# Transposed right-side sums and a Strassen opening for the up matrix

## The chip, the cores and the metric

The kernel runs on one core of one Trainium2 chip. The metric is the device time of one execution in microseconds (us), the median of three runs. The engines have these names in the profile: PE is the tensor engine (matrix products and transposes into PSUM), DVE the vector engine, ACT the scalar engine, POOL the GpSimd engine, SP the engine that issues most DMAs. SBUF is the working memory, PSUM the eight banks into which TensorE adds up its products.

## The reference, cut to what matters

One decoder layer on 1024 rows of width 1024. The change touches only the two gated feed-forward blocks, one at the start and one at the end:

```python
def swiglu(h, w_gate, w_up, w_down):
    return (jax.nn.silu(h @ w_gate) * (h @ w_up)) @ w_down

x = x + 0.5 * swiglu(rms_norm(x, g_ffn1), w1_gate, w1_up, w1_down)
...   # projections, two attentions, gates, output projection
x = x + 0.5 * swiglu(rms_norm(x, g_ffn2), w2_gate, w2_up, w2_down)
```

The gate and up matrices are 1024 x 2816, all in float32.

## The kernel before

**Numbers.** A float32 operand is held as two fp32r parts, high and low (`halve`, L375 to L379: the scalar engine copies the high part, POOL or the vector engine subtracts it to get the low part). A block product (`times`, L465 to L471) is four steps over the inner dimension with three matmuls each: 12 matmuls of 128x128 by 512 columns into one PSUM bank.

**Feed-forward, first half** (`ffn_in`, L446). The weights are the left side, taken two blocks of 128 columns at a time, so eleven pairs p, for gate (e = 0) and up (e = 1). Each left side is cut into four blocks A11, A12, A21, A22 (two column blocks, two halves of the inner dimension). The right side is the normalised input, transposed, cut into B11, B21 (rows 0 to 511 of x) and B12, B22 (rows 512 to 1023). In pairs 1 to 10, `products` (L477) takes seven Strassen products in place of eight block products; `FACTORS` (L371) gives their operands, with S1 to S4 from the left blocks (`left_sides`, L452) and T1 to T4 from the right ones. T1 = B12 - B11, T2 = B22 - T1, T3 = B22 - B12, T4 = B21 - T2.

**The opening** (`opening`, L501) is pair 0, where the right side isn't ready yet. It is written out by hand for TensorE, DVE, ACT and POOL: the `manual_schedule` block keeps each engine in program order. Before the change both matrices are multiplied there with eight plain block products each (`half(e, r, c, q)`), column by column of the result, and `gated` multiplies silu of gate (`gate`) with up. Between the products stand the turns: `Right.turn` (L419) makes one right-side operand out of 16 TensorE transposes of rows into four PSUM banks and four high and four low parts. T1 to T4 are formed in the row layout (`Right.sum`, L430, four subtractions each) and then turned as B12 and B22 are. B11 and B21 are turned ahead of the products: in the first block right there, in the second one inside the output projection before it (`between`, L2112). `Right.stat` and `Right.norm` (L405, L411) normalise a row tile.

**What sets the order around it.** The eight PSUM banks are four letters with two buffers each (`banks`, L323). A new tile of a letter waits until an older one has been read for the last time. Left-side operands come from nine tiles in turn (`op`), weights as loaded from four (`raw`), the transposed operands from 28 (`tt`), working tiles of 512 columns from `ct` and `sums`. Outside the hand-written opening a planner orders each engine's instructions. `lefts` (L596) loads and splits the left side of the next product group, called as `nxt` within the opening. `finish` (L587) forms the operands of the second half and stores them. The second half (`ffn_out`, L618) multiplies with the down matrix in four passes. Between the two feed-forward blocks lie the projections and the attentions, about 670 to 1540 us.

Of the kernel before, what the change touches and what calls it, by code (L numbers as in the profile page):

```python
# [11 lines left out]
F32R = mybir.dt.float32r  # L12
# [45 lines left out]
def f32(ap):  # L58
    return ap.bitcast(F32)
# [186 lines left out]
def trunk(ctx, tc, x, positions, g_ffn1, w1_gate, w1_up, w1_down, g_mix, w_in, g_cq, w_uq_a, w_q_idx,  # L246
# [134 lines left out]
    class Right:  # L381
# [4 lines left out]

        ROWS = {"B11": (0, 0), "B21": (0, 1), "B12": (1, 0), "B22": (1, 1), "T1": (0, 0), "T2": (0, 0), "T3": (0, 0),
                "T4": (0, 1)}

        def __init__(self, g, bank, gains, ct, tt, nm):  # L390
            self.g, self.bank, self.gains, self.ct, self.tt, self.nm = g, bank, gains, ct, tt, nm
            self.B, self.y, self.gB = {}, {}, None
# [5 lines left out]
        def place(self, xs, half, junk=None):  # L398

            self.x, self.half, self.junk, self.rs = xs, half, junk, {}  # L400
            for q in range(2):
                self.y[half, q] = ([xt[:, q * 512:q * 512 + 512] for xt in xs] if half else
                                   [self.ct(f"{self.nm}y{q}{t}") for t in range(4)])

# [10 lines left out]

        def operand(self, n):
            self.B[n] = [self.tt(f"{self.nm}{n}{k}") for k in range(4)]

        def turn(self, n, letters="abcd"):  # L419

            rows = self.y[self.ROWS[n]]
            if n not in self.B:
                self.operand(n)
            for k in range(4):
                ps = self.bank("pst", letters[k % len(letters)])
                for j in range(4):
                    nc.tensor.transpose(ps[:, j * P:(j + 1) * P], rows[j][:, k * P:(k + 1) * P], ident)
                halve(self.B[n][k], ps, nc.vector)

        def sum(self, n):  # L430

            b11, b21, b12, b22 = (self.y[h, q] for h in range(2) for q in range(2))
            out, a, b = {"T1": (b11, b12, b11), "T3": (b11, b22, b12), "T2": (b11, b22, b11), "T4": (b21, b21, b11)}[n]
            for j in range(4):
                nc.vector.tensor_sub(out[j], a[j], b[j])

# [9 lines left out]
    def ffn_in(nm, R, wg, wu, raw, op, sums, ct, bank, staged, rows, first=None, beside=lambda n, ins: None):  # L446
# [54 lines left out]
        def opening(raws, rows, nxt):  # L501


            A = [dict(zip(("A11", "A12", "A21", "A22"), (r[:, q] for r in rs for q in (HI, LO)))) for rs in raws]
            O = ({}, {})

            def left(e, *names):
                for n in names:
                    O[e][n] = halve(op(f"{nm}{e}0{n}"), A[e][n])

            ps, sg = {}, {}

            def half(e, r, c, q):

                letter = "abcd"[r + 2 * c]
                if not q:
                    ps[e, r, c] = bank(f"p{letter}", letter)
                times(O[e][f"A{r + 1}{q + 1}"], B[f"B{q + 1}{c + 1}"], ps[e, r, c], not q)

            def gate(r, c):  # L520
                sg[r, c] = ct(f"{nm}sg")
                nc.scalar.activation(sg[r, c], ps[0, r, c], AF.Silu)

            def gated(r, c):
                nc.vector.tensor_mul(sg[r, c], sg[r, c], ps[1, r, c])

            if "B11" not in B:
                left(0, "A11")
                R.operand("B12")
                R.turn("B11")  # L530
                left(0, "A12")
                R.turn("B21")
                left(0, "A21", "A22")
                R.second()
            else:
                left(0, "A11", "A12", "A21", "A22")
            for t, n in enumerate(("A11", "A12", "A21", "A22")):
                if 4 - t <= len(rows):
                    R.stat(rows[t + len(rows) - 4])
                left(1, n)  # L540
# [60 lines left out]
        for p in range(NF // 2):  # L601
            if not p:
                first = first or [[load(w, q, f"{nm}{e}r0") for q in range(2)] for e, w in enumerate((wg, wu))]
                with tc.manual_schedule(engines={e.engine for e in (nc.tensor, nc.vector, nc.scalar, nc.gpsimd)}):
                    H, S, nxt = opening(first, rows, lambda: lefts(1, 0))
            else:
                for e, w in enumerate((wg, wu)):
                    u, nxt = products(nxt, f"{nm}{e}", lambda: lefts(p + e, 1 - e, True))
                    if not e:
                        H = silu(u)  # L610
                for a, b in zip(H, u):
                    nc.vector.tensor_mul(a, a, b)
                S = u[1:]
            finish(p, H, S)

# [146 lines left out]
    with tc.tile_pool(name="ring1", bufs=1) as rpool, tc.tile_pool(name="s1", bufs=1) as spool, tc.tile_pool(name="ps1", bufs=1, space=PSUM) as psum:  # L762
# [3 lines left out]
        with tc.tile_pool(name="t1", bufs=1, side="right") as tpool, tc.tile_pool(name="c1", bufs=1) as cpool:  # L766
            tt = of(tpool, "t", 28, dt=F32R)
            fp = lambda place: lambda name: f32(place(name))
# [3 lines left out]
            early, late = fp(in_turn((c3, 3), (c1, 1))), pair  # L772
            R = Right(g_ffn1, bank, fp(op), fp(in_turn((c5, 5), (c3, 3))), tt, "a")
            xs = []
# [35 lines left out]
            def rows(t):  # L810
                xs.append(fp(tt)(f"x{t}"))
                nc.sync.dma_start(xs[t], x[0, t * P:(t + 1) * P, :])
# [1211 lines left out]
    with tc.tile_pool(name="ring2", bufs=1) as rpool, tc.tile_pool(name="ps6", bufs=1, space=PSUM) as psum:  # L2024
        op, raw = ring(rpool)
        bank = banks(psum)
        with tc.tile_pool(name="m0", bufs=1) as mpool:
# [18 lines left out]
            tpool = ctx2.enter_context(tc.tile_pool(name="t2", bufs=1, side="right"))  # L2046
            tt = of(tpool, "t", 28, dt=F32R)
            fp = lambda place: lambda name: f32(place(name))

            def residual(half):  # L2050
                xs = []
                for q in range(4):
                    xs.append(fp(tt)(f"x2{half}{q}"))
                    t = 4 * half + q
# [52 lines left out]
        with tc.tile_pool(name="c2", bufs=1) as cpool:  # L2107
            ct = of(cpool, "c", NC_, 512)
            x1 = residual(1)
            R = Right(g_ffn2, bank, fp(op), ct, tt, "b")  # L2110

            def between():  # L2112
                R.operand("B12")
                R.turn("B11")
                R.turn("B21")

# [64 lines left out]
```

## Time and profile before

| what | us |
|---|---|
| median of three runs | 2219.55 (2217.72 to 2219.59) |
| the profiled execution | 2216.6 |
| its span, first to last instruction | 2214.8 |
| mean granted TensorE clock | 0.995 of full speed |
| first opening's first product, next pair's first product | 21.26, 76.24 |
| second opening's, the same two | 1562.06, 1616.16 |

A row of the timeline gives the start, the time from the first start to the last end of the merged instructions, the engine, the line, what is written and read, the shape and the count; in brackets the idle time ahead and what ended it. Names are the program's: `a` and `b` in front mark the first and second block, then `B` and `T` are right-side operands, `A` and `S` left-side ones, `pst` a bank of transposes, `pa` to `pd` banks of products. A row of stretches gives the length, then busy time and count for PE, PEld (loading of weights, beside PE), DVE, ACT and POOL, the granted clock, the share of the DMA engines and GB/s. A row of waits gives who waited on whom, the sum in us, how often, and the longest.

### The profile page before, as it was taken

To read this page: it belongs to the slowest core of one execution; us is meant where nothing else is said; L and a number is where in the kernel's file an instruction comes from. 1 tells how busy PE (TensorE), PEld (TensorE's weight loads), DVE (VectorE), ACT (ScalarE), POOL (GpSimd) and SP (SyncE) were. 2 spreads that over 40 slices of the span, in tenths; PEclk is the share of its full clock that TensorE was granted. 3 is DMA by queue.
4 is the path that set the end of the run, shared out by engine and by line. 5 is a ranking of instruction groups with operands and counts; after the bars stand their busy time and mean duration, and the time that the engine had idled before them with its cause. 6 is when DMAs were issued, how large, how long until landed. Compare 5 with 4: busy or idle time off the path is not lost.

```text
span 2214.8 us, 30577 instructions
## 1 busy us (share of the span) xinstructions
PE 2156.8 (97%) x10460; PEld 1800.9 (81%) x10460; DVE 1524.3 (69%) x2548; ACT 1103.8 (50%) x2169; POOL 858.1 (39%) x698
## 2 busy tenths in 40 slices
PE   7999999999999999899999899999999999999999
PEld 6888888888879888688788688878888888888877
DVE  5575767688874598677787687754565555678685
ACT  5333333335454358999987565533333232233443
POOL 3355555523245445211111322264255554552233
PEclk9999999999999999999999999999999999999999
DMA  5487878497675343665654522565133232359655
GB/s 172 94 252 204 243 215 232 169 318 248 213 196 165 112 143 110 202 178 156 168 166 161 199 91 94 204 226 198 63 99 106 94 109 95 113 171 326 225 167 186
DMA packets 269052, 381.01 MB, mean 172 GB/s; under 512 B 23264, under 2 KB 157040, under 8 KB 268896
## 3 DMA queue, kind: packets, MB, share of 16 engines
q1 hardware_dynamic: 256384, 339.17, 49.7%
q0 software_dynamic: 12512, 39.89, 4.9%
q8 instruction: 82, 1.34, 0.3%
q14 instruction: 74, 0.61, 0.1%
HBM read 259.94 MB, written 119.05 MB: 171 GB/s over the span
## 4 chain that ended last, share of the span: by engine, by line
PE 80%; ACT 7%; DVE 6%; DMA 3%; issue 2%; POOL 1%; SPq 0%; ACTq 0%; DVEq 0%; POOLq 0%
PE p L681 6%; PE p L682 6%; PE p L680 5%; PE pc L468 4%; PE pd L468 4%; PE pd L469 4%; PE pd L470 4%; PE pc L469 4%; PE pc L470 4%; PE pa L468 3%; PE pa L469 3%; PE pa L470 3%; ACT junka L1194 3%; PE psf L308 2%; PE psf L309 2%
## 5 line engine op out<-in xcount | busy, mean ns | idle before, releaser
L1194 ACT ACTIVATE junka<-u,cand,sig 128x768 bf16<-128x768 f32 (+4 forms) x186 | 183.7, 988 | 5.6 <-DVE cand L1191 4.0
L1635 DVE TENSOR_TENSOR_SCAN left<-left 128x640 f32<-128x640 f32 (+3 forms) x64 | 86.3, 1349 | 4.0 <-ACT left L1627 4.0
L802 ACT ACTIVATE swh<-swr 128x512 fp32r<-128x512 f32 x48 | 30.2, 628 | 117.2 <-issue 47.8
L1128 POOL DMA_DIRECT2D gd<-evg x32 | 17.9, 561 | 152.6 <-ACT evg L1125 112.8
L803 DVE TENSOR_TENSOR swr<-swr,swh 128x512 f32<-128x512 f32 x48 | 41.1, 856 | 43.0 <-ACT swh L802 42.9
L1684 DVE TENSOR_TENSOR pt<-pstT,pt 128x512 fp32r<-128x512 f32 (+1 forms) x96 | 50.8, 550 | 28.6 <-ACT pt L1682 28.3
L584 ACT ACTIVATE b0u<-b0u 128x512 f32<-128x512 f32 x20 | 12.7, 633 | 95.2 <-DVE b0u L491 78.9
L1684 DVE TENSOR_TENSOR pt<-pspT,pt 128x512 fp32r<-128x512 f32 x72 | 46.8, 684 | 16.3 <-ACT pt L1682 16.3
L1682 ACT ACTIVATE pt<-pspT 128x512 fp32r<-128x512 f32 x72 | 39.7, 596 | 29.2 <-PE pspT L1894 29.2
L681 PE MATMUL p<-bT,bS 128*128 128x512 f32 x132 | 51.5, 390 | 2.8 <-DVE bT L378 2.8
L1815 ACT ACTIVATE e<-e,nm 128x256 f32<-128x256 f32 (+7 forms) x64 | 49.3, 773 | 9.6 <-DVE nm L1810 9.4
L1548 DVE SCALAR_TENSOR_TENSOR u<-relu,WI,u 128x512 f32<-128x512 f32 (+1 forms) x70 | 50.1, 734 | 5.0 <-ACT relu L1541 4.4
L1803 DVE CUSTOM_DVE_ANT_0 e<-psL,bias 128x512 f32<-128x512 f32 (+3 forms) x96 | 49.7, 550 | 5.3 <-PE psL L1840 5.3
L682 PE MATMUL p<-bT,bS 128*128 128x512 f32 x132 | 51.1, 390 | 1.0 <-POOL bS L378 1.0
L681 PE MATMUL p<-aT,aS 128*128 128x512 f32 x132 | 51.4, 389 | 0.0
L1638 DVE TENSOR_TENSOR sa<-sa,left 128x639 f32<-128x639 f32 (+3 forms) x64 | 48.1, 753 | 3.7 <-ACT sa L1629 0.2
L682 PE MATMUL p<-aT,aS 128*128 128x512 f32 x132 | 50.4, 389 | 0.0
L1541 ACT ACTIVATE relu<-psdot 128x512 f32<-128x512 f32 (+1 forms) x80 | 40.1, 520 | 17.9 <-DVE u L1548 8.6
L1682 ACT ACTIVATE pt<-pstT 128x512 fp32r<-128x512 f32 (+1 forms) x96 | 47.0, 518 | 3.3 <-PE pstT L1738 3.1
L1894 PE MATMUL pspT<-ident,e 128*128 128x128 f32 x288 | 39.6, 277 | 8.3 <-DVE ri L1817 5.5
L1629 ACT ACTIVATE sa<-psz 128x512 f32<-128x512 f32 (+2 forms) x96 | 47.0, 511 | 0.1
L1627 ACT ACTIVATE left<-psz 128x512 f32<-128x512 f32 (+2 forms) x96 | 46.2, 506 | 1.6 <-PE psz L1662 1.4
(3021 smaller groups left out, 8228.9 us busy)
## 6 DMA issues: line engine op xcount, KB each, us to landing
aw<-in_w_down_dram SPq DMA_DIRECT2D x33, 512.0 KB, 5.2
bw<-in_w_down_dram SPq DMA_DIRECT2D x33, 512.0 KB, 4.9
swr<-in_w_in_dram SPq DMA_DIRECT2D x48, 256.0 KB, 6.0
a0r<-in_w_gate_dram SPq DMA_DIRECT2D x22, 512.0 KB, 7.1
a1r<-in_w_up_dram SPq DMA_DIRECT2D x22, 512.0 KB, 7.7
b0r<-in_w_gate_dram SPq DMA_DIRECT2D x22, 512.0 KB, 4.2
b1r<-in_w_up_dram SPq DMA_DIRECT2D x22, 512.0 KB, 3.9
x<-in_x_dram SPq DMA_DIRECT2D x16, 512.0 KB, 6.3
```

Source lines behind the costliest of these rows:

```text
L468: nc.tensor.matmul(ps, a[:, c], b[k][:, HI], start=start and k == 0, stop=False, skip_group_check=True)
L469: nc.tensor.matmul(ps, a[:, c], b[k][:, LO], start=False, stop=False, skip_group_check=True)
L470: ins = nc.tensor.matmul(ps, a[:, l], b[k][:, HI], start=False, stop=k == 3, skip_group_check=True)
L680: nc.tensor.matmul(ps[q][m], S[:, h], T[:, HI], start=p == 0, stop=False)
L681: nc.tensor.matmul(ps[q][m], S[:, h], T[:, LO], start=False, stop=False)
L682: nc.tensor.matmul(ps[q][m], S[:, l], T[:, HI], start=False, stop=p == last)
L1194: nc.scalar.activation(junks[1][:, 0:(i + 1) * P], score[i], AF.Sign, scale=sig[:, b:b + 1], bias=cand.bitcast(F32)[:, b:b + 1], accum_out ...
L1548: nc.vector.scalar_tensor_tensor(ac, r, wv, ac, op0=ALU.mult, op1=ALU.add)
L1635: nc.vector.tensor_tensor_scan(back, back, back, 1.0, op0=ALU.mult, op1=ALU.bypass)
L1682: nc.scalar.activation(pt[:, off:512], tp[:, off:512], AF.Copy)
L1684: nc.vector.tensor_sub(pt[:, 512 + off:1024], tp[:, off:512], f32(pt[:, off:512]))
L1803: nc.vector.tensor_tensor_reduce(e[:, c], lp[:, 0:n_], bias[:, c], 1.0, LOW, op0=ALU.add, op1=ALU.max, accum_out=m)
```

## The change

The sums T1 to T4 are formed after the transposition: B11 and B21 are kept as raw float32 copies when they are turned, T1 is taken from the banks of B12 (`less` in `turn`), T2 from those of B22, T3 and T4 from raw tiles. Their high and low parts come from SBUF (`low`). So only B11, B21, B12 and B22 are turned. Pair 0 multiplies the gate matrix by eight block products as before, and the up matrix by the seven products, in the order 1, 2, 6, 5, 7, 3, 4. The raw copies use four of the 28 transposed tiles (`ts`) and working tiles. The up side needs S1 to S4: two sums on DVE, two on POOL.

```diff
-        def sum(self, n):
-            b11, b21, b12, b22 = (self.y[h, q] for h in range(2) for q in range(2))
-            out, a, b = {"T1": (b11, b12, b11), "T3": (b11, b22, b12), "T2": (b11, b22, b11), "T4": (b21, b21, b11)}[n]
-            for j in range(4):
-                nc.vector.tensor_sub(out[j], a[j], b[j])
...
             for k in range(4):
                 ps = self.bank("pst", letters[k % len(letters)])
                 for j in range(4):
                     nc.tensor.transpose(ps[:, j * P:(j + 1) * P], rows[j][:, k * P:(k + 1) * P], ident)
                 halve(self.B[n][k], ps, nc.vector)
+                if less:
+                    nc.vector.tensor_sub(less[0][k], ps, less[1][k])
+                out.append(ps)
+            return out
+
+        def keep(self, copies, eng=None):
+            for t, ps in copies:
+                if eng is nc.vector:
+                    nc.vector.tensor_copy(t, ps)
+                else:
+                    nc.scalar.activation(t, ps, AF.Copy)
+
+        def less(self, to, a, b):
+            for t, p, q in zip(to, a, b):
+                nc.vector.tensor_sub(t, p, q)
...
+        def low(self, n, eng):
+            if n not in self.B:
+                self.operands(n)
+            for t, r in zip(self.B[n], self.raw[n]):
+                nc.scalar.activation(t[:, HI], r, AF.Copy)
+            for t, r in zip(self.B[n], self.raw[n]):
+                eng.tensor_tensor(t[:, LO], r, f32(t[:, HI]), op=ALU.subtract)
...
+            S = {n: sums(f"{nm}s{n}") for n in ("S1", "S2", "S3", "S4")}
+            A11, A12, A21, A22 = (A[1][n] for n in ("A11", "A12", "A21", "A22"))
+            nc.vector.tensor_add(S["S1"], A21, A22)
+            nc.vector.tensor_sub(S["S2"], S["S1"], A11)
+            A[1].update(S)
             for t in rows:
                 R.norm(t)
-            half(0, 0, 0, 0)
-            half(0, 0, 0, 1)
+            half(0, 0, 0, "a")
+            half(0, 0, 1)
             gate(0, 0)
-            half(0, 1, 0, 0)
-            half(0, 1, 0, 1)
+            left(1, "S2")
+            half(1, 0, 0, "b")
+            pa = bank("pa", "a")
+            up(1, pa)
+            u2 = ct(f"{nm}u2")
+            half(1, 0, 1)
+            nc.scalar.activation(u2, pa, AF.Copy)
             gate(1, 0)
-            half(1, 0, 0, 0)
-            R.turn("B12", "cd")
-            half(1, 0, 0, 1)
-            R.sum("T1")
-            gated(0, 0)
-            R.turn("B22", "cd")
-            half(1, 1, 0, 0)
-            half(1, 1, 0, 1)
-            gated(1, 0)
-            half(0, 0, 1, 0)
-            R.turn("T1", "ab")
-            half(0, 0, 1, 1)
+            left(1, "S1")
+            up(2, pa, False)
+            R.turn("B12", "cdab", (r["T1"], r["T3"]))
+            nc.gpsimd.tensor_sub(S["S3"], A11, A21)
+            nc.gpsimd.tensor_sub(S["S4"], A12, S["S2"])
+            left(1, "S3")
+            R.less(r["T2"], R.turn("B22", "bcdc"), r["T1"])
+            R.low("T1", nc.gpsimd)
+            half(0, 1, 0, "d")
+            half(1, 1, 0, "b")
+            R.low("T2", nc.vector)
+            left(1, "S4", "A22")
+            half(0, 1, 1)
             gate(0, 1)
-            R.sum("T2")
-            half(0, 1, 1, 0)
-            R.turn("T2", "ab")
-            half(0, 1, 1, 1)
+            half(1, 1, 1)
             gate(1, 1)
-            R.sum("T4")
-            R.sum("T3")
-            half(1, 0, 1, 0)
-            half(1, 0, 1, 1)
-            R.turn("T3", "ab")
-            gated(0, 1)
+            R.less(r["T3"], r["T2"], r["T3"])
+            pb = bank("pb", "b")
+            up(6, pb)
+            R.low("T3", nc.vector)
+            nc.vector.tensor_add(u2, u2, pb)
+            R.less(r["T4"], r["T4"], r["T2"])
+            pd = bank("pd", "d")
+            up(5, pd)
+            u3 = ct(f"{nm}u3")
+            nc.vector.tensor_add(u3, u2, pd)
+            pc = bank("pc", "c")
+            up(7, pc)
+            R.low("T4", nc.vector)
+            nc.vector.tensor_mul(sg[0, 0], sg[0, 0], pa)
+            nc.vector.tensor_add(u3, u3, pc)
             nxt = nxt()
-            half(1, 1, 1, 0)
-            half(1, 1, 1, 1)
-            R.turn("T4", "ab")
-            gated(1, 1)
-            return [sg[0, 0], sg[0, 1], sg[1, 0], sg[1, 1]], [ct(f"{nm}s{n}") for n in range(3)], nxt
+            up(3, pd, False)
+            c12 = ct(f"{nm}c12")
+            nc.vector.tensor_add(c12, u2, pd)
+            up(4, pc, False)
+            nc.vector.tensor_add(u2, u2, pc)
+            return [sg[0, 0], sg[0, 1], sg[1, 0], sg[1, 1]], (None, c12, u2, u3), nxt
...
             def between():
-                R.operand("B12")
-                R.turn("B11")
-                R.turn("B21")
+                R.operands("B12")
+                R.kept()
+                R.kept2()
+                R.keep(zip(R.raw["T3"], R.turn("B11")))
+                R.keep(zip(R.raw["T4"], R.turn("B21")))
```

`half(r, c, q)` is now gate's alone, and `up(n, bank, start)` is Strassen product n of the up matrix. In the first opening the raw copies are made on DVE (`R.keep(..., nc.vector)`, between the statistics of the row tiles), in the second on ACT. Of the up side's left blocks A21 is no longer split, and S1 to S4 are. `finish` takes the working tiles of the up sums as its own.

More of the change, by code (lines that the diff above doesn't have):

```diff
@@ L381, in trunk, with __init__ @@
     class Right:
[L387 to L391, printed above, removed]
+        ROWS = {"B11": (0, 0), "B21": (0, 1), "B12": (1, 0), "B22": (1, 1)}
+        def __init__(self, g, bank, gains, yt, ct, tt, ts, spare, nm):
+            self.g, self.bank, self.gains, self.yt, self.ct = g, bank, gains, yt, ct
+            self.tt, self.ts, self.spare, self.nm = tt, ts, spare, nm
             self.B, self.y, self.gB = {}, {}, None
@@ L414, in norm, with operands, turn @@
                 nc.vector.scalar_tensor_tensor(out_, xt[:, c], self.rs[t], self.gB[:, c], op0=ALU.mult, op1=ALU.mult)
[L416 to L421, printed above, removed]
+        def operands(self, *ns):
+            for n in ns:
+                self.B[n] = [(self.ts if n == "T4" else self.tt)(f"{self.nm}{n}{k}") for k in range(4)]
+        def turn(self, n, letters="abcd", less=None):
             if n not in self.B:
-                self.operand(n)
+                self.operands(n)
+            rows, out = self.y[self.ROWS[n]], []
             for k in range(4):
@@ L511, in opening, with half, up @@
             ps, sg = {}, {}
-            def half(e, r, c, q):
-                letter = "abcd"[r + 2 * c]
+            def half(r, c, q, letter=None):
                 if not q:
-                    ps[e, r, c] = bank(f"p{letter}", letter)
-                times(O[e][f"A{r + 1}{q + 1}"], B[f"B{q + 1}{c + 1}"], ps[e, r, c], not q)
+                    ps[r, c] = bank("pg", letter)
+                times(O[0][f"A{r + 1}{q + 1}"], B[f"B{q + 1}{c + 1}"], ps[r, c], not q)
             def gate(r, c):
                 sg[r, c] = ct(f"{nm}sg")
-                nc.scalar.activation(sg[r, c], ps[0, r, c], AF.Silu)
-            def gated(r, c):
-                nc.vector.tensor_mul(sg[r, c], sg[r, c], ps[1, r, c])
+                nc.scalar.activation(sg[r, c], ps[r, c], AF.Silu)
+            def up(n, ps_, start=True):
+                a, b = FACTORS[n]
+                times(O[1][a], B[b], ps_, start)
             if "B11" not in B:
                 left(0, "A11")
-                R.operand("B12")
-                R.turn("B11")
+                R.operands("B12", "B11", "B21", "B22", "T1")
+                R.kept()
+                copies = list(zip(R.raw["T3"], R.turn("B11")))
                 left(0, "A12")
-                R.turn("B21")
+                R.keep(copies[0:1], nc.vector)
+                p21 = R.turn("B21")
+                R.kept2()
+                copies += zip(R.raw["T4"], p21)
                 left(0, "A21", "A22")
@@ L535, in opening @@
             else:
+                copies = []
+                R.operands("B22", "T1")
                 left(0, "A11", "A12", "A21", "A22")
-            for t, n in enumerate(("A11", "A12", "A21", "A22")):
+            for t, n in enumerate((("A11",), ("A12",), (), ())):
+                R.keep(copies[1 + 2 * t:3 + 2 * t], nc.vector)
                 if 4 - t <= len(rows):
                     R.stat(rows[t + len(rows) - 4])
-                left(1, n)
+                left(1, *n)
+            r = R.raw
@@ L604, in ffn_in @@
                 with tc.manual_schedule(engines={e.engine for e in (nc.tensor, nc.vector, nc.scalar, nc.gpsimd)}):
-                    H, S, nxt = opening(first, rows, lambda: lefts(1, 0))
+                    H, u, nxt = opening(first, rows, lambda: lefts(1, 0))
             else:
@@ L810, in rows @@
             def rows(t):
-                xs.append(fp(tt)(f"x{t}"))
+                xs.append(fp(tt if t > 3 else ts)(f"x{t}"))
                 nc.sync.dma_start(xs[t], x[0, t * P:(t + 1) * P, :])
@@ L2109, in trunk @@
             x1 = residual(1)
-            R = Right(g_ffn2, bank, fp(op), ct, tt, "b")
+            R = Right(g_ffn2, bank, fp(op), ct, ct, tt, ts, in_turn((sums, 3), (ct, 1)), "b")
             def between():
-                R.operand("B12")
-                R.turn("B11")
-                R.turn("B21")
+                R.operands("B12")
+                R.kept()
+                R.kept2()
+                R.keep(zip(R.raw["T3"], R.turn("B11")))
+                R.keep(zip(R.raw["T4"], R.turn("B21")))
             R.gain()
```

23 lines of the change are left out of this document (15 added, 8 removed).

## The prediction

> **What bounds the kernel now.** I read the page first (busy times), then the busy time of the two openings by stretch, then TensorE's waits, then the order of instructions inside an opening.
>
> ```profile
> span 2214.8 us, 30577 instructions
> PE 2156.8 (97%) x10460; PEld 1800.9 (81%) x10460; DVE 1524.3 (69%) x2548; ACT 1103.8 (50%) x2169; POOL 858.1 (39%) x698
> ...
> 21.26:76.24 54.98, 54.43 (x291) 46.24 (x289) 35.40 (x54) 25.50 (x48) 15.65 (x13) 1.00 0.21 53
> 1562.06:1616.16 54.10, 54.10 (x290) 46.17 (x288) 29.67 (x46) 19.80 (x37) 12.60 (x11) 1.00 0.18 54
> ...
> PE p L681 <- DVE aB L378: 1.1, 2, 0.8
> PE p L680 <- ACT ahalf L693: 0.5, 1, 0.5
> ...
> PE p L681 <- DVE bT L378: 2.8, 1, 2.8
> PE p L682 <- POOL bS L378: 1.0, 1, 1.0
> ```
>
> The two rows of the stretches run from the first product of each opening to the first product of the next pair; columns are length, then busy time of PE, PEld, DVE, ACT, POOL. TensorE is busy for 54.43 of 54.98 us and for all 54.10 us. So both openings are bound by TensorE's own instruction stream. The last four rows are all of TensorE's waits from the end of the first opening to 700 us (two rows) and from the end of the second to the last instruction (two): none in the other ten pairs of either, 1.6 and 3.8 us in the output stages. What an opening saves is therefore carried on behind it. The profiled execution took 2216.6 us (span 2214.8), 2.95 us under the median 2219.55; I work out a difference and subtract it from the median.
>
> **What goes from TensorE.** Its pace:
>
> ```profile
> 1562.06 0.39 PE L468 MATMUL pa<-bB,b00A 128*128 128x512 f32 x1
> ...
> 1567.49 0.39 PE L468 MATMUL pb<-bB,b00A 128*128 128x512 f32 x1
> ...
> 1575.66 1.91 PE L427 MATMUL pst<-ident,x 128*128 128x128 f32 x16
> 1577.32 0.48 PE L468 MATMUL pa<-bB,b10A 128*128 128x512 f32 x1
> ```
>
> Two block products (24 matmuls) take 5.43 us, so one takes 2.72. One turn of 16 transposes takes 1577.32 - 1575.66 = 1.66. An opening has 16 block products and six turns between them; 16 x 2.72 + 6 x 1.76 (with re-entry) = 54.1, which is the second stretch. After the change there are 8 products for gate and 7 for up, and only B12 and B22 are turned. Gone: 2.72 + 4 x 1.76 = **9.8 us per opening**. In the first opening a 0.55 us wait goes too:
>
> ```profile
> 29.01 6.94 DVE L414 SCALAR_TENSOR_TENSOR x<-x,rs,ag 128x1024 f32<-128x1024 f32 x4
> 36.00 1.64 PE L427 MATMUL pst<-ident,x 128*128 128x128 f32 x13 [0.55 <-DVE x L414]
> ```
>
> The B12 turn now follows six products rather than five, so it starts at 21.26 + 6 x 2.72 = 37.6 us. The four norms, 0.8 us later behind S1 and S2, with one POOL subtraction beside them instead of two, end near 36.1; cover 1.5 us. The raw copies of B11 and B21 (8 a time; vector in the first opening, scalar in the second) sit ahead of that, where both engines wait for input. No row shows such a vector copy (PSUM to SBUF, one operand); between nothing and the 0.68 of a vector instruction of that size I take 0.60, and nothing waits. Second opening:
>
> ```profile
> 1537.42 4.03 ACT L377 ACTIVATE bB<-pst 128x512 fp32r<-128x512 f32 x8 [5.00 <-PE pst L427]
> ...
> 1540.20 0.48 PE L308 MATMUL psout<-wout110h,m 128*128 128x512 f32 x1
> ```
>
> The scalar copies, 0.50 each, stand behind B11's four high parts, so the first bank of B11 is read at about 1540.0, and the output product wants it at 1540.2: cost 0 to 0.1.
>
> **What comes onto the vector engine.** The forecast rests on its queue from the B12 turn on. I call the start of that turn t0 (37.6 and 1578.4 us). Rows for the durations:
>
> ```profile
> 1576.29 2.07 ACT L377 ACTIVATE bB<-pst 128x512 fp32r<-128x512 f32 x4 [2.56 <-PE pst L427]
> ...
> 1576.92 2.48 DVE L378 TENSOR_TENSOR bB<-pst,bB 128x512 fp32r<-128x512 f32 x4 [4.71 <-ACT bB L377]
> 1579.33 2.49 DVE L435 TENSOR_TENSOR by<-x,by 128x512 f32<-128x512 f32 x4
> ...
> 78.02 2.55 POOL L378 TENSOR_TENSOR a01A<-a0r,a01A 128x512 fp32r<-128x512 f32 x2
> ```
>
> Vector: 0.60 us a tile from one to the next, whether an operand lies in PSUM (L378) or both in SBUF (L435). Scalar 0.52. POOL 1.27. The first vector instruction of a turn starts 1576.92 - 1575.66 = 1.26 after the turn. But vector and POOL disturb each other:
>
> ```profile
> 117.59 1.67 DVE L589 TENSOR_TENSOR a1u<-a0u,a0u 128x512 f32<-128x512 f32 x1
> 119.18 1.77 DVE L591 TENSOR_TENSOR a1u<-asg,a0u 128x512 f32<-128x512 f32 x1
> 120.88 1.77 DVE L590 TENSOR_TENSOR a1c<-a1u,asg 128x512 f32<-128x512 f32 x1
> ...
> 118.67 1.74 POOL L378 TENSOR_TENSOR a02A<-a0r,a02A 128x512 fp32r<-128x512 f32 x1
> 120.37 1.73 POOL L378 TENSOR_TENSOR a02S<-a02s,a02S 128x512 fp32r<-128x512 f32 x1
> ...
> 77.65 2.48 DVE L378 TENSOR_TENSOR aT<-pst,aT 128x512 fp32r<-128x512 f32 x4 [3.24 <-ACT aT L377]
> ```
>
> With both operands in SBUF, vector and POOL alternate, one each per 1.70 us: a collision costs the vector engine 1.70 - 0.60 = 1.1 us. Reading PSUM (last row, beside the POOL row at 78.02) it isn't touched.
>
> The vector queue behind t0 + 1.26, in its written order: B12 low and T1 in turn (8), B22 low (4), T2 (4), T2 low (4), T3 (4), T3 low (4), u2 += pb, T4 (4), u3 = u2 + pd, T4 low (4), sg x pa, u3 += pc. These are 40 instructions, 24.0 us, with no gap: each scalar high part comes at 0.52 and is ready. POOL meets it: the last T1 low falls on the first T2 low (0.35), the lows of S4 and A22 on T2's lows (1.1 each; their scalar copies come behind T2's), the next pair's A11 low on T4's lows (1.1). The other T1 lows run beside PSUM readers and collide with nothing. Together 3.65 us. So u3 = u2 + pd ends at t0 + 24.2 and u3 += pc at t0 + 29.0.
>
> TensorE beside it: two turns, 3.34; wait for the bank of B12's second tile (read last at t0 + 3.76), 0.55; then seven products (four of gate, up 6, 5, 7), each with its operand ready: t0 + 22.9. Up 3 adds into pd, which u3 = u2 + pd must have read: it starts at t0 + 24.4, **wait 1.5**. Up 4 adds into pc, which u3 += pc must have read: t0 + 29.2 instead of 27.1, **wait 2.05**. Queued behind the last vector additions are only the next pair's sums, whose products come 2.7 us behind up 4 and later. The opening ends at t0 + 31.9, that is 6 x 2.72 + 31.9 = 48.2 us after its first product.
>
> What else issues: POOL gets S3, S4, four T1 lows and three more left-side lows (9 x 1.27 on 15.65 us), scalar three more high parts and u2 (4 x 0.52 on 25.50): 27 and 28 of 48 us. The DMAs stay the same in number, but the loads of the next up blocks move:
>
> ```profile
> 32.90 1.96 POOL L378 TENSOR_TENSOR a10A<-a1r,a10A 128x512 fp32r<-128x512 f32 x1
> ...
> a1r<-in_w_up_dram SPq DMA_DIRECT2D x22, 512.0 KB, 7.7
> ...
> 89.56 0.69 DVE L457 TENSOR_TENSOR a11s<-a1r 128x512 f32<-128x512 f32 x1
> ```
>
> Their buffer is free behind A22's low part, now at t0 + 15 = 52.6 instead of 34.9 us. Landing 7.7 us later, near 60, they are wanted near 89.6 - 6.75 = 82.8: hidden by 22 us.
>
> **Sum:** first opening 54.98 - 48.2 = 6.75; second 54.10 - 48.2 = 5.85; together **12.6 us**: 2219.55 - 12.6 = **2207.0** (the profiled execution: 2204.0).
>
> [...]
>
> **The rivals.**
> *B, the vector engine keeps up:* the POOL lows fall into gaps. Then up 3 and up 4 find their banks read, the opening takes 15 x 2.72 + 3.34 + 0.55 = 44.7 us, and 10.3 + 9.4 = 19.7 are gained: 2199.9. For it: few collisions; against: the queue of 24 us alone, without a collision, is longer than TensorE's 21.8 (eight products) beside it, so that few us of collisions show.
> *C, the waits slow TensorE's clock.*
>
> ```profile
> 907.14 0.66 PE L1514 MATMUL psqt<-ident,qx 128*128 128x128 f32 x4 [2.71 <-DVE qx L1510]
> ...
> 907.00:910.00 3.00, 2.86 (x15) 2.45 (x16) 1.03 (x5) 2.97 (x6) 0.00 (x0) 1.00 1.01 270
> ...
> 1492.53 0.80 PE L309 MATMUL psout<-wout010l,m 128*128 128x512 f32 x1 [2.41 <-POOL wout010l L297]
> 1493.12 0.63 PE L310 MATMUL psout<-wout010h,m 128*128 128x512 f32 x1
> ...
> 1495.68 0.46 PE L308 MATMUL psout<-wout010h,m 128*128 128x512 f32 x1
> 1495.97 0.40 PE L309 MATMUL psout<-wout010l,m 128*128 128x512 f32 x1
> ```
>
> Behind a wait of 2.41 us the matmuls came at 0.43 instead of 0.23 us for 3.15 us, a loss of 1.5; behind one of 2.71 the granted clock stayed 1.00. A wait of 2.05 lies below both, with little room. Price 3.0 in all: gain 9.6, 2210.0. [...]
> *D, more collisions:* all seven POOL lows meet the vector queue, 7.7 instead of 3.65 us; the wait passes 2.4 us and brings C's price. Gain 12.6 - 8.1 - 3.0 = 1.5: 2218, no change.
> *E, slower:* everything outside the openings is ordered by a planner whose times shift, and in the output stages TensorE has once hung on a staged block:
>
> ```profile
> 618.26 11.48 DMA aS310r<-staged
> ```
>
> If a new plan puts one more such load late in each output stage, that is 2 x 11.5 - 12.6, 10 us slower: 2230. It decides from 17 us lost, so from two such hits; against it, that stage waits 1.6 us now.
>
> **How the numbers follow.** Chances: forecast 0.48, B 0.16, C 0.18, D 0.11, E 0.07. The range must leave out no more than D and E (0.18): from B's 2199.9, less 1 us for the bounds of the copies and the unread banks, to C's 2210 with up to 4 us of D's collisions: 2199 to 2214. A measurement here tells about 0.2% (4.4 us) from no change. Faster by more: forecast, B, C, 0.82. Within: D, 0.11. Slower: E, 0.07.
>
> **What would show it.** TensorE has 152 instructions less (twice 12 matmuls and 64 transposes), the first opening from its first product to the next pair about 48.2 us, the second the same. The steps: vector instructions 0.60 apart behind t0 + 1.26, a few of 1.7 beside POOL lows of S4, A22 and A11; TensorE's waits on the vector engine ahead of up 3 and up 4, 1.5 and 2.05 us; the granted clock 1.00. Wrong if T2's or T3's low parts make up 6 or up 7 wait, if the pair behind an opening waits for its left sides, or if the openings shorten and the output stages lengthen.

## The result, and the profile after

| | before | after |
|---|---|---|
| median, us | 2219.57 (2217.72 to 2220.78, 4 runs) | 2195.94 (2193.52 to 2198.58, 4 runs) |
| profiled execution | 2216.6 | 2196.82 |
| ratio of the medians | | 0.9898, 95% interval 0.9886 to 0.9909 |

The change gains 23.6 us where 12.6 were forecast; the time lies 3 us below the range. The two profiled executions are 19.8 us apart. That is the 19.7 of rival B, but it is made up otherwise, as the next view shows.

From the page of the kernel after, the busy times (its span is 2195.0 us):

```profile
PE 2138.5 (97%) x10308; PEld 1784.8 (81%) x10308; DVE 1539.4 (70%) x2562; ACT 1114.7 (51%) x2185; POOL 887.8 (40%) x716
```

There are 152 TensorE instructions fewer, as counted ahead.

The most useful view is the busy time by stretch, with the cuts laid at the same instructions in both kernels: the first product of an opening, and the first product of the output stage behind it. So the rows are the first pass over the eleven pairs of column blocks, everything in the middle (the first output stage among it), the second pass, and the second output stage. Columns are length, then busy time of PE, PEld, DVE, ACT, POOL, the granted clock, the DMA share and GB/s. Before:

```profile
21.26:457.16 435.90, 435.35 (x1971) 361.65 (x1969) 297.05 (x378) 165.79 (x301) 226.59 (x152) 1.00 0.68 196
457.16:1562.06 1104.90, 1068.87 (x5570) 897.88 (x5569) 806.50 (x1633) 702.94 (x1452) 346.93 (x343) 0.99 0.55 174
1562.06:1997.05 434.99, 434.99 (x1969) 361.68 (x1968) 256.54 (x322) 134.18 (x242) 213.06 (x150) 1.00 0.34 109
1997.05:2210.90 213.85, 210.01 (x925) 173.06 (x923) 152.15 (x198) 89.91 (x158) 66.11 (x42) 1.00 0.68 225
```

After:

```profile
21.46:448.67 427.21, 426.10 (x1896) 352.62 (x1894) 305.35 (x388) 169.08 (x305) 238.54 (x161) 1.00 0.67 199
448.67:1554.20 1105.53, 1069.24 (x5570) 899.87 (x5568) 802.69 (x1633) 706.94 (x1460) 354.13 (x343) 0.99 0.55 174
1554.20:1981.28 427.08, 425.96 (x1894) 352.53 (x1892) 263.50 (x326) 137.33 (x246) 230.36 (x159) 1.00 0.35 112
1981.28:2191.20 209.92, 209.78 (x925) 173.20 (x923) 155.62 (x196) 90.52 (x158) 59.32 (x42) 1.00 0.68 228
```

The first pass is 8.69 us shorter, the second 7.91. The middle is 0.63 longer. The second output stage, which the change does not touch, is 3.93 shorter: TensorE is busy there for the same 210 us, and it no longer waits. With a start 0.20 us later this gives 8.69 - 0.63 + 7.91 + 3.93 - 0.20 = 19.7.

TensorE's waits after, in the first opening (two rows), the second opening (two) and the first output stage (one); in the second output stage there is none:

```profile
PE pd L497 <- DVE au L622: 0.8, 1, 0.8
PE pg L497 <- DVE araw L431: 0.2, 1, 0.2
...
PE pd L497 <- DVE bu L622: 0.8, 1, 0.8
PE pg L497 <- DVE braw L431: 0.2, 1, 0.2
...
PE p L737 <- DVE aT L378: 1.1, 1, 1.1
```

The wait ahead of up 3 is there at half its forecast size. The one ahead of up 4 is missing. TensorE's timeline says why (the turns of B12 and B22, the first product behind them, up 3, and two products behind it):

```profile
37.90 3.66 PE L428 MATMUL pst<-ident,x 128*128 128x128 f32 x32
41.80 0.47 PE L497 MATMUL pg<-aB,a00A 128*128 128x512 f32 x1 [0.24 <-DVE araw L431]
...
61.90 0.50 PE L497 MATMUL pd<-aB,a10S 128*128 128x512 f32 x1 [0.78 <-DVE au L622]
...
64.75 0.39 PE L497 MATMUL pa<-aB,a01A 128*128 128x512 f32 x1
...
67.87 0.39 PE L497 MATMUL pc<-aT,a10A 128*128 128x512 f32 x1
```

Read the tile names: `a01A` at 64.75 is the left side of the next pair, so this is its first product. It stands between up 3 and up 4 (`a10A` at 67.87). The block written by hand keeps only its own instructions in order; the planner may put others between them. So the opening has to be measured to the end of up 4 with one product (2.72 us) taken out:

```profile
21.46:70.59 49.13, 48.02 (x228) 39.45 (x226) 45.03 (x68) 30.92 (x56) 28.30 (x22) 1.00 0.25 61
1554.20:1603.20 49.00, 47.88 (x226) 39.37 (x224) 36.76 (x53) 25.01 (x45) 27.62 (x20) 1.00 0.19 60
```

49.13 - 2.72 = 46.4 and 49.00 - 2.72 = 46.3 us, where 48.2 were forecast and 54.98 and 54.10 stood before.

The product of the next pair is itself late: it takes 67.87 - 64.75 = 3.12 us instead of 2.72. Its third matmul is the first to use the low part of A11, and the loading of weights stood for it (here and once more in the second opening):

```profile
PEld pa L499 <- POOL a01A L378: 0.5, 1, 0.5
```

So 0.4 us of the 46.4 are a wait of the next pair's for its left side.

The vector queue beside it, and the POOL rows that meet it:

```profile
46.35 2.47 DVE L446 TENSOR_TENSOR ar<-pst,araw 128x512 f32<-128x512 f32 x4
48.74 3.58 DVE L464 TENSOR_TENSOR aT<-ar,aT 128x512 fp32r<-128x512 f32 x4
52.25 3.58 DVE L446 TENSOR_TENSOR araw<-ar,araw 128x512 f32<-128x512 f32 x4
55.76 2.49 DVE L464 TENSOR_TENSOR aT<-araw,aT 128x512 fp32r<-128x512 f32 x4
...
61.17 0.68 DVE L622 TENSOR_TENSOR au<-au,pd 128x512 f32<-128x512 f32 x1
61.77 2.49 DVE L464 TENSOR_TENSOR aT<-ar,aT 128x512 fp32r<-128x512 f32 x4
...
64.78 0.67 DVE L627 TENSOR_TENSOR au<-au,pc 128x512 f32<-128x512 f32 x1
```

```profile
50.09 1.69 POOL L378 TENSOR_TENSOR a10S<-asS,a10S 128x512 fp32r<-128x512 f32 x1 [1.35 <-ACT a10S L377]
51.74 1.74 POOL L378 TENSOR_TENSOR a10A<-a1r,a10A 128x512 fp32r<-128x512 f32 x1
62.59 2.82 POOL L378 TENSOR_TENSOR a01A<-a0r,a01A 128x512 fp32r<-128x512 f32 x1 [9.11 <-ACT a01A L377]
```

Four vector instructions take 2.47 to 2.49 us undisturbed. Two groups take 3.58, one collision of 1.1 each, with the low parts of S4 and A22. The low part of the next pair's A11 at 62.59 falls on T4's low parts, as forecast, but there the vector engine loses nothing (2.49) and POOL takes 2.82 instead of 1.27; it ends at 65.41, and that is what the weights above waited for. In these rows four vector instructions that read PSUM (2.47 us at 46.35) are undisturbed beside T1's low parts on POOL (5.07 us for four from 43.67, 1.27 each), and the only ones disturbed (3.58 us) have both inputs in SBUF. Which of the two engines is held the rows do not settle: at 50.09 and at 62.59 alike POOL's row starts inside a running vector instruction, and yet the next vector instruction was held in one place (1.1 us) and POOL in the other (2.82 us instead of 1.27).

### The profile page after: what moved, and what is told of

Same layout as the page of the kernel before. It is cut to its first block, busy times and chain, and to the rows that moved or that the text cites. A ratio compares the mean times of both kernels' runs of the same rounds, so it can differ in the third digit from the quotient of the medians.

```text
span 2195.0 us, 30360 instructions
## 1 busy us (share of the span) xinstructions
PE 2138.5 (97%) x10308; PEld 1784.8 (81%) x10308; DVE 1539.4 (70%) x2562; ACT 1114.7 (51%) x2185; POOL 887.8 (40%) x716
## 4 chain that ended last, share of the span: by engine, by line
PE 79%; ACT 7%; DVE 7%; issue 4%; DMA 2%; POOL 1%; SPq 0%; DVEq 0%; ACTq 0%; POOLq 0%
PE p L737 6%; PE p L738 6%; PE p L736 6%; ACT junka L1250 4%; PE pa L499 3%; PE pa L497 3%; PE pa L498 3%; PE pc L499 3%; PE pc L497 3%; PE pc L498 3%; PE pd L499 3%; PE pd L497 3%; PE pd L498 3%; PE psf L308 2%; PE psf L309 2%
## 5 line engine op out<-in xcount | busy, mean ns | idle before, releaser
L1950 PEld LDWEIGHTS pspT<-ident,e 128*128 128x128 f32 x288 | 34.6, 143 | 15.8 <-issue 5.9
```

What stands on the lines that cost most here:

```text
L1950: nc.tensor.transpose(tp[:, q * P:(q + 1) * P], E[n + q][:, j * P:(j + 1) * P], ident)
```

## The experiments

Theory: the two openings give 8.7 + 7.9 us, by TensorE's work less short waits behind the vector queue; the rest comes from waits of the second output stage that the new order of its instructions happens to miss. Rivals: those waits are an accident of one execution; the seven products or the turns alone make the gain; the vector queue isn't what TensorE waits for.

All lengths below are of the four stretches shown above, cut at the same instructions, in one profiled execution of each kernel. Each ratio is taken against runs of the kernel before in the same set.

| run | median, us | ratio to before | first pass | middle | second pass | second output stage |
|---|---|---|---|---|---|---|
| before | 2217.26 to 2219.57 in four sets of runs | | 435.90 | 1104.90 | 434.99 | 213.85 |
| after | 2195.94 | 0.9898 | 427.21 | 1105.53 | 427.08 | 209.92 |
| e1 before again | one run, 2219.11 | | 435.96 | 1106.77 | 435.00 | 215.17 |
| e2 first opening only | 2208.98 | 0.9956 [0.9941, 0.9970] | 427.25 | 1104.62 | 435.00 | 214.28 |
| e3 plain up | 2218.46 | 1.0003 [0.9993, 1.0012] | 437.00 | 1104.95 | 435.67 | 213.93 |
| e4 after again | 2195.68 | 0.9898 [0.9881, 0.9914] | 427.25 | 1104.97 | 427.10 | 209.86 |
| e5 up 4 first | 2196.56 | 0.9898 [0.9881, 0.9915] | 427.79 | 1108.01 | 427.66 | 210.22 |
| e6 POOL early | 2192.61 | 0.9884 [0.9869, 0.9899] | 426.23 | 1107.61 | 425.62 | 209.94 |
| e7 POOL early, up 4 first | 2196.30 | 0.9899 [0.9884, 0.9913] | 426.77 | 1106.08 | 426.00 | 211.15 |
| e8 plain up, other order | 2202.80 | 0.9935 [0.9922, 0.9949] | 428.44 | 1107.12 | 428.34 | 214.14 |
| e9 before, one low part moved | 2213.70 | 0.9983 [0.9974, 0.9992] | 435.90 | 1103.96 | 435.00 | 209.46 |

Read the columns before the times. Where two kernels have the same opening, the length of a pass agrees within 0.1 us. The middle scatters over 4 us (1103.96 to 1108.01), by 1.9 us for the kernel before alone (1104.90, 1106.77). So a few tenths in an opening can be read from a pass, and can't from a median.

**e1, the kernel before once more.**

> The kernel before, once more, for a second profile. Question: TensorE waits 1.6 us in the first output stage and 3.8 us in the second (2.8 us of it behind a GpSimd subtraction that took 7.4 us at 2127.23), and the changed kernel waits 1.1 and 0 there. Theory A: these waits come with the order in which the instructions stand, so they recur: 1.6 and 3.8 us, within 0.5. Rival B: they are an accident of that execution: the second stage waits under 1.5 us here, and its profile is about 3 us nearer to the changed kernel's.

The waits of its second output stage, and from the timeline the POOL instruction ahead of them:

```profile
PE p L681 <- DVE bT L378: 2.6, 1, 2.6
PE p L682 <- POOL bS L378: 1.0, 1, 1.0
```

```profile
2128.50 7.39 POOL L378 TENSOR_TENSOR bS<-bS33r,bS 128x512 fp32r<-128x512 f32 x1 [7.51 <-ACT bS L377]
```

They recur, 3.6 us after 3.8, and the 7.4 us of one POOL instruction to a hundredth. Theory A holds: it comes with the order of the instructions, not with the execution. (In the first stage 1.7 us after 1.6.) The stage is 1.3 us longer than in the first profile all the same, because behind the wait of 2.6 us TensorE's granted clock was halved for 3.12 us (the number after POOL's busy time):

```profile
2150.22:2153.34 3.12, 3.12 (x8) 2.50 (x8) 3.12 (x6) 0.00 (x0) 0.00 (x0) 0.51 0.39 114
```

Behind the same wait in the first profile, 2.83 us long, it stayed at 1.00. In the kernel after, the same subtraction stands beside other vector instructions:

```profile
2109.70 1.67 POOL L378 TENSOR_TENSOR bS<-bS33r,bS 128x512 fp32r<-128x512 f32 x1 [4.84 <-ACT bS L377]
```

**e2, only the first opening changed.**

```diff
-H, u, nxt = opening(first, rows, lambda: lefts(1, 0))
+H, u, nxt = (opening if nm == "a" else old_opening)(first, rows, lambda: lefts(1, 0))
...
-R = Right(g_ffn2, bank, fp(op), ct, ct, tt, ts, in_turn((sums, 3), (ct, 1)), "b")
+R = OldRight(g_ffn2, bank, fp(op), ct, tt, "b")
```

(`old_opening` and `OldRight` are those of the kernel before; `between` and the second block's tiles go back to it too.)

> The first opening as changed, the second as before. Theory A (each stage's gain belongs to the order of its own block): the first opening, from its first product to the end of up 4 less the one product of the next pair inside it, takes 46.4 us and the first output stage is 1.4 us shorter, as in the changed kernel; the second opening takes 54.1 us and its output stage still waits 3 to 4 us; the whole is 7 to 10 us below before. Rival B (the waits of the second output stage depend on when that stage begins): they go here too, and the whole is 11 to 14 us below before.

Its median is 8.6 us below that of before (2217.58 in these runs). The first pass is that of the changed kernel (427.25), the second that of before (435.00), and in its second output stage the waits are still there:

```profile
PE p L872 <- DVE bT L378: 2.7, 1, 2.7
PE p L873 <- POOL bS L378: 1.0, 1, 1.0
```

Theory A: beginning that stage 10 us earlier doesn't remove them; the changed second opening does. What theory A said of the first output stage is borne out by half: it is about 0.8 us shorter than before, not 1.4, and TensorE waits 1.5 us there (1.6 before, 1.1 in the changed kernel).

**e3, only the transposed sums, up by eight plain products.**

```diff
 half(1, 0, 0, "b")
-pa = bank("pa", "a")
-up(1, pa)
+upper(0, 0, 0, "a")
...
-pb = bank("pb", "b")
-up(6, pb)
+upper(1, 0, 0, "b")
+upper(1, 0, 1)
 R.low("T3", nc.vector)
...
+upper(0, 1, 0, "d")
+upper(0, 1, 1)
...
+upper(1, 1, 0, "c")
+upper(1, 1, 1)
```

(`upper(r, c, q)` is a plain block product of the up matrix; S1 to S4 and the sums of the seven products go, and each of the four results is multiplied with silu of gate as before.)

> Only the first half of the change: the sums T1 to T4 in the transposed layout, but up by eight plain products. Theory A (TensorE's instructions add up, and the vector queue holds nobody here, because T4 is first wanted by the next pair): an opening takes 16 products of 2.72, two turns of 1.67 and the 0.24 us bank wait, 47.1 us, to the next pair's first product; that is 7.9 and 7.0 us less than before. The seven products then are worth only 47.1 - 46.4 = 0.7 us an opening of the 2.72 us that TensorE loses in work less 0.94 of wait, or up to 1.8 if the turns cost less here. Rival B: the vector queue holds TensorE here as well, and the opening takes 48 us or more; the seven products then carry 2 us or more each. In time: 2219.6 - 14.9 = 2204.7, or as low as 2199 if the waits of the output stages go as they do in the changed kernel.

A miss: 14.9 us were expected and nothing came (1.0003). TensorE's waits at the next pair, and from the timeline the scalar row that starts the delay:

```profile
PE pa L497 <- ACT a01A L377: 3.2, 1, 3.2
...
PE pa L499 <- POOL a01A L378: 2.1, 1, 2.1
```

```profile
63.46 0.63 ACT L462 ACTIVATE aT<-araw 128x512 fp32r<-128x512 f32 x1 [11.01 <-PE pu L499]
```

T3's first tile takes the buffer of B12's first tile. In this order the last plain product that reads B12 ran near the end of the opening, so the scalar engine stood still for 11.01 us and the high parts of T3 came late, then T4's, then those of the next pair's left side behind them on the scalar engine. Neither theory had this. And the waits are not the whole price. Behind the two of them the granted clock is 0.50:

```profile
74.20:79.48 5.28, 5.28 (x12) 4.13 (x13) 5.18 (x7) 4.03 (x8) 3.26 (x3) 0.50 0.00 0
```

Matmuls come 0.43 us apart there instead of 0.23, which costs about 2.6 us more. Waits (3.2 + 2.1) and slow matmuls are 7.9 of the 8.6 us by which this first pass is longer than that of e8, which differs from it only in the order of the plain products. The changed kernel escapes this: gate's products are the last readers of B12 there.

**e8, the same with the readers of B12 first.**

```diff
 R.low("T2", nc.vector)
+upper(0, 1, 0, "a")
+upper(1, 1, 0, "c")
 half(0, 1, 1)
...
-upper(1, 0, 0, "b")
-upper(1, 0, 1)
+upper(0, 1, 1)
 R.low("T3", nc.vector)
+upper(1, 1, 1)
...
+upper(1, 0, 0, "b")
+upper(1, 0, 1)
```

> The plain-up kernel again (sums in the transposed layout, up by eight plain products), with its products in another order: those that read B12 come first, because T3's first tile takes B12's buffer, and the vector queue stood still for 11.6 us in the run before until the last reader of B12 was through; the next pair's left side then came 5.3 us late. Theory A: with B12 free about 6 us earlier the opening takes 47.1 to 47.6 us to the next pair's first product, the wait ahead of that product is below 0.5 us, and the first pass over the column blocks is 7 to 8 us shorter than before (435.7), near 428: the four turns are then worth 7 to 8 of the 8.7 us, the seven products 1. Rival B: T3 still comes late (its tile freed at t0 + 18), the pair behind waits 1 us or more, and the gain of the turns alone is below 6.5 us an opening.

Theory A, near its upper edge. The first product at 20.36 and the next pair's at 68.00 are 47.6 us apart, with no wait at the second:

```profile
20.36 0.47 PE L497 MATMUL pg<-aB,a00A 128*128 128x512 f32 x1 [0.19 <-DVE araw L439]
...
68.00 0.39 PE L497 MATMUL pa<-aB,a01A 128*128 128x512 f32 x1
```

Against e1 the passes are 435.96 - 428.44 = 7.5 and 435.00 - 428.34 = 6.7 us shorter: that is what the four turns are worth. The seven products add 428.44 - 427.21 = 1.2 and 428.34 - 427.08 = 1.3, not the 2.72 of a block product: the rest goes into the wait ahead of up 3 (0.94 against the pace of the product before it, and 0.1 in slower first matmuls) and into the late low part of A11 (0.4); none of these stands in e8. The second output stage still has its waits (214.14).

**e4 and e5, the kernel after again, and with the next pair's first product held behind up 4.**

```diff
-        def times(a, b, ps, start=True):
+        def times(a, b, ps, start=True, pinned=False):
...
+                if pinned and k == 0:
+                    tc.keep_in_program_order(ins)
...
-lambda: lefts(p + e, 1 - e, True))
+lambda: lefts(p + e, 1 - e, True), p == 1 and not e)
```

> The changed kernel, once more, for a second profile and a closer ratio on the chip of the next three. Theory: its waits stand in the order of its instructions and recur: 0.24 us ahead of the first product behind the turns, 0.78 us ahead of up 3, none ahead of up 4, 1.1 us in the first output stage and none in the second; 0.9898 of before, within 0.001. Rival: the waits of the output stages come back (up to 3.8 us) and the ratio is 0.9915.

> The first product of the next pair is held behind up 4 on TensorE, where the prediction had it; the changed kernel runs it ahead of up 4. Theory A (the vector queue is late by what the trace shows: its last addition ends 65.46 at a start of 37.9 for the turns, and up 3 ends at 64.75): up 4 waits 0.7 to 1.0 us, and each opening ends that much later, 47.2 us instead of 46.4, 1.6 us in all. Prediction on record: 2.05 us of wait each, 4.1 us in all. Rival: the wait is hidden elsewhere, and the time does not differ from the changed kernel's by more than 0.5 us.

e4 gives the same waits as the first run of this kernel (0.8 and 0.2 in each opening, 1.0 in the first output stage, none in the second) and the same ratio. In e5 a wait appears ahead of up 4; in the first opening:

```profile
PE pc L497 <- DVE au L629: 0.7, 1, 0.7
```

The passes are 0.54 and 0.56 us longer than in e4, 1.1 us in all, where theory A had 1.6 and the prediction 4.1. So the planner's placing saves 0.55 us an opening: it hides the wait ahead of up 4, and pays 0.4 us for A11's late low part, which behind up 4 has come in time. The other 1.4 us of the forecast 2.05 weren't there to be saved.

**e6, the low parts of S4 and A22 ahead of T1's on POOL.**

```diff
             for t in rows:
                 R.norm(t)
+            nc.vector.tensor_sub(S["S3"], A11, A21)
+            nc.vector.tensor_sub(S["S4"], A12, S["S2"])
...
-            left(1, "S1")
+            left(1, "S1", "S3", "S4")
...
-            nc.gpsimd.tensor_sub(S["S3"], A11, A21)
-            nc.gpsimd.tensor_sub(S["S4"], A12, S["S2"])
-            left(1, "S3")
+            left(1, "A22")
...
-            left(1, "S4", "A22")
```

(The operand tiles of up's A11 and A12 are also taken first in the turn of nine, so that S4 and A22 follow them and not gate's.)

> The low parts of S4 and A22 on GpSimd are moved ahead of those of T1, beside vector instructions that read PSUM (S3 and S4 themselves are taken on the vector engine while it is idle ahead of the turns, and up's first two left sides are given other buffers so that S4 and A22 need not wait for gate's). Theory A (two collisions of 1.1 us are what makes the vector queue late): the eight instructions that took 3.58 us a group of four take 2.4 to 2.5, the vector queue ends 2.2 us earlier, up 3 no longer waits (0.78 us now, 0.94 with its re-entry), and each opening takes 45.4 us instead of 46.4: 1.9 us below the changed kernel. Rival B: T1's low parts on GpSimd are pushed back into T2's on the vector engine, and the same or a longer wait stands ahead of up 3; no gain.

The same two vector groups, and from TensorE's timeline the first product behind the turns and up 3:

```profile
49.01 2.48 DVE L464 TENSOR_TENSOR aT<-ar,aT 128x512 fp32r<-128x512 f32 x4
51.42 2.49 DVE L446 TENSOR_TENSOR araw<-ar,araw 128x512 f32<-128x512 f32 x4
```

```profile
42.07 0.47 PE L497 MATMUL pg<-aB,a00A 128*128 128x512 f32 x1 [0.57 <-DVE araw L431]
...
61.19 0.39 PE L497 MATMUL pd<-aB,a10S 128*128 128x512 f32 x1
```

No collision, and up 3 starts without a wait. The passes are 1.0 and 1.5 us shorter than in e4, though 0.3 us is given back in the first opening, where the high part of S4 now delays those of B12 (0.57 us of wait behind the turns, 0.24 before). The weights of the next pair no longer wait either: A11's low part is ready at 64.04, and the matmul that needs it starts at 64.37. So the collisions are what makes the vector queue late. Against e8 the seven products are now worth 428.44 - 426.23 = 2.2 and 428.34 - 425.62 = 2.7 us, nearly their full 2.72. The median is 3.1 us below e4's; the intervals of the two ratios overlap, so that this is the fastest kernel of the study rests on the passes, not on the times.

**e7, both edits.**

> Both edits of the two runs before. Theory A: with the collisions gone the vector queue ends before up 3 does, so that holding the next pair's product behind up 4 costs nothing: the same as the run before within 0.3 us an opening, no wait ahead of up 3 or up 4. Rival B: up 4 waits for something else than the vector queue, 0.7 us or more.

A little of the wait is left, up 4's first product on TensorE and the row of the vector queue behind it:

```profile
63.74 0.47 PE L497 MATMUL pc<-aT,a10A 128*128 128x512 f32 x1 [0.16 <-DVE au L629]
```

```profile
53.89 2.50 DVE L464 TENSOR_TENSOR aT<-araw,aT 128x512 fp32r<-128x512 f32 x4 [0.49 <-ACT aT L462]
```

The passes are 0.54 and 0.38 us longer than in e6, so theory A is missed by a tenth or two. With the collisions gone, T3's low parts stand 0.49 us for their high parts: on the scalar engine these come behind gate's last Silu, which starts at 52.74 when its product is done. Rival B's 0.7 isn't reached. The second output stage has 1.1 us of waits on the vector engine again (211.15), and e5's 0.5, with no starved subtraction: what stands there goes with the order of each plan.

**e9, the kernel before with one instruction moved.**

```diff
-return (left("S3", p), halve(t3, a, V))
+return (left("S3", p, V if nm == "b" and p == 3 else None), halve(t3, a, V))
```

> The kernel before with one instruction moved: the low part of S3 of pair 3 in the second output stage goes from GpSimd to the vector engine. On GpSimd it took 7.4 us in four kernels of four whose second opening isn't the changed one, against 1.3 to 1.7 us elsewhere. Theory A (that one instruction makes the 3.6 to 3.8 us of waits behind it): TensorE's waits in the second output stage fall below 0.5 us, that stage takes 209.6 to 210.5 instead of 213.6 to 214.9 us, and the whole is about 4 us below before, with nothing of the openings touched. Rival B: the load or the vector engine is late there anyhow; 2 us of the wait or more stay.

The second output stage by stretch, and from the timeline the next POOL instruction:

```profile
1995.64:2205.10 209.46, 209.46 (x925) 173.24 (x923) 151.17 (x197) 90.25 (x158) 64.36 (x41) 1.00 0.68 228
```

```profile
2129.88 5.76 POOL L378 TENSOR_TENSOR bS<-bS34r,bS 128x512 fp32r<-128x512 f32 x1 [11.58 <-ACT bS L377]
```

TensorE is busy for all of it. The stage is 4.4 us shorter than before, a little more than theory A had, and the median is 3.6 us below that of before (2217.26 in these runs). Theory A: about 4 us of the change's gain can be had without the change, by one subtraction on another engine. The next POOL instruction takes 5.76 us in its place, but nobody needs it soon enough to wait.

## Why the prediction was wrong

**What held.** The bound, and TensorE's pace: the turns are worth 7.5 and 6.7 us (forecast 4 x 1.76 = 7.04, and 0.55 of a wait in the first opening). The start of the turns, t0, lies 16.44 us behind the first product (16.3 forecast). The vector engine keeps 0.60 us a tile from SBUF and from PSUM alike (2.49 and 2.47 for four). The wait ahead of up 3 is where it was put, behind u3 = u2 + pd. The loads and the copies stayed hidden.

**First step that failed: "wait 2.05" ahead of up 4.** Nothing of it is there. About 1.4 us of it never were: u3 += pc ends 65.45 - 37.90 = 27.55 us behind t0 instead of 29.0. That is the term "together 3.65" of collisions, mis-sized: 2.2 were paid. The collision with A11's low part was paid by POOL, and T1's last low part ended just as T2's first began. The other 0.55 us is what the planner gained by putting the next pair's first product there (e5). The prediction took the order in the source for the order on the engine.

**Second, smaller: "wait 1.5" ahead of up 3** was 0.78, or 0.94 against the pace of the product before it. Up 3 started at t0 + 24.0 and not 24.4, as the 0.35 us for T1's last low part were not paid, and TensorE was ready for it at t0 + 23.1 and not 22.9. (The bank wait counted as 0.55 was 0.24, but the turns took as much longer: the product behind them starts at t0 + 3.90, where 3.34 + 0.55 = 3.89 were summed.)

**Against these**, one sign of being wrong came true that the prediction had named: the pair behind the opening waited for its left side, 0.4 us, because POOL paid for the collision with A11's low part and TensorE paid behind POOL. Together the opening came out at 46.4 instead of 48.2 us: 2.05 and 0.4 less, 0.4 more, and 0.1 more each for the later t0 and the slower first matmuls of up 3. The passes show 8.69 and 7.91 where 6.75 and 5.85 were summed: 4.0 us of the error.

**Third: the second output stage.** Its 3.8 us of waits were quoted and then left standing in the sum, as if what the change does not touch kept its waits; rival E asked only whether that stage could get worse. All instructions outside the openings are ordered anew, and a wait that hangs on one starved subtraction can go as well as come. It went: 3.9 us, which e1, e2, e8 and e9 tie to that instruction. That the new order misses it is luck of the plan, as far as the runs show; what in the changed second opening makes the planner order that stage otherwise was not followed further.

12.6 + 4.0 + 3.9 = 20.5 us are accounted for by stretches. The medians give 23.6, and 22.8 in the second set of runs; the intervals of the two ratios reach down to gains of 20.2 and 19.1, so no further cause is needed, and none was found. The range ended at 2199 because its lower edge was B's opening with no word for the output stages. The openings' 16.6 us alone would have given 2203, inside it; what took the time below was that lucky stage and the scatter of the rest.

**The rivals.** B (the vector engine keeps up) is not what happened, though its 19.7 fits the two profiled executions: up 3 still waits, and only e6 comes near B's opening (its first is 48.15 - 2.72 = 45.4 us by the same measure, against 44.7). C did not occur: the granted clock is 1.00 in both openings, with no wait there over 0.8 us. Such a drop does occur in this kernel, though: the clock fell to 0.50 behind the waits of e3, and to 0.51 behind one of 2.6 us in e1. D had too many collisions. E had the wrong sign, and its price was misread: the row at 618.26 is a transfer of 11.48 us on the chain of work, and TensorE has no wait between 616 and 635 us in that run.

## What to carry to other kernels

Cut both profiles at the same instructions and compare stretch lengths before explaining a time: the passes here agree within 0.1 us while the middle moves by 4. A block written in order fixes only its own instructions, so a wait forecast inside it may be filled by the planner from behind; and when the rest is planned anew, the waits standing elsewhere are terms of the sum too, with either sign. Where a buffer, or another engine at work on SBUF at the same time, makes an engine late (here 3.58 us for four instructions instead of 2.48), moving the other party beside instructions that read PSUM (e6), or freeing the buffer earlier (e8), can be worth as much as the arithmetic saved (e6: 1.0 and 1.5 us a pass, where the seven products alone gained 1.2 and 1.3) or far more (e8 against e3: 8.6 and 7.3).

## What the runs showed of the hardware

A POOL subtraction on SBUF that meets back-to-back vector subtractions on SBUF does not always alternate with them. At 50.09 and 51.74 it did (1.69 and 1.74 us); at 62.59 it took 2.82 us, held past the last two of T4's low parts, and in e1 7.39, held past some ten. Each case recurs in its place: 7.39 or 7.40 us in before, e1 and e2, with the same waits behind it in e3 and e8 (2.8 and 1.0 us), and 2.79 to 2.82 at the low part of the next pair's A11 in the first opening of after, e3, e5, e6, e7 and e8. What decides is open. The moment of POOL's arrival alone does not: e2 has both outcomes with POOL 0.43 us into a vector instruction. Vector rows first (the second instruction of the pair at 2116.27 starts 0.60 behind it), then POOL's:

```profile
1994.08 0.69 DVE L838 TENSOR_TENSOR bt<-bw,bt 128x512 f32<-128x512 f32 x1
1994.69 1.78 DVE L378 TENSOR_TENSOR bT<-bt,bT 128x512 fp32r<-128x512 f32 x1
...
2116.27 1.28 DVE L861 TENSOR_TENSOR x<-x,bhalf 128x512 f32<-128x512 f32 x2
2117.47 0.68 DVE L861 TENSOR_TENSOR bhalf<-bhalf,bhalf 128x512 f32<-128x512 f32 x1
```

```profile
1994.51 1.41 POOL L378 TENSOR_TENSOR bS<-bS23r,bS 128x512 fp32r<-128x512 f32 x1 [4.62 <-ACT bS L377]
...
2117.30 7.40 POOL L378 TENSOR_TENSOR bS<-bS33r,bS 128x512 fp32r<-128x512 f32 x1 [7.51 <-ACT bS L377]
```

The length of a wait alone does not tell whether TensorE's granted clock drops behind it; what else decides is open. At one place of the same kernel it stayed at 1.00 behind 2.83 us (before) and fell to 0.51 for 3.12 us behind 2.6 (e1).
